# Booking more time for every transfer in a list scheduler that orders a decoder trunk's instructions

## The chip, the cores and the metric

The kernel runs on one core of a Trainium2 chip. The metric is the device time of one launch in microseconds (us). Three timed runs of the kernel before gave 1246.37, 1246.60 and 1246.83 us; the median is 1246.6 us.

## The reference

One inference step of a two-layer decoder trunk with width 1024, on a prompt of 512 tokens and on 8 sequences of 8 sample tokens, all in float32:

```python
for l in range(DEPTH):                                     # DEPTH = 2
    sh1, sc1, g1, sh2, sc2, g2 = ada_mod(c, ada_w[l], ada_b[l], 6)
    h = modulate(rms_norm(x, norm_g[l, 0]), sh1, sc1)
    if l < N_A_LAYERS:                                     # layer 0
        out, nbuf, h_last = recurrent_block(h, ...)
    else:                                                  # layer 1
        q = apply_partial_rope((h @ attn_w_q[j]).reshape(...), pos)
        out = sliding_sink_attention(q, k_all, v_all, attn_sinks[j], p0) @ attn_w_o[j]
    x = x + g1[:, None, :] * out
    h = modulate(rms_norm(x, norm_g[l, 1]), sh2, sc2)
    x = x + g2[:, None, :] * swiglu(h, ffn_w_in[l], ffn_w_out[l])
    if l == N_A_LAYERS - 1:                                # shared keys and values, once
        hk = modulate(rms_norm(x, kv_norm_g), kv_shift, kv_scale)
        kv = (hk @ w_kv).reshape(B, T, 2, N_KV_HEADS, HEAD_DIM)
        ...
y = rms_norm(x, final_g)
```

`swiglu(h, w_in, w_out)` is `(silu(gate) * up) @ w_out` with `gate, up` the halves of `h @ w_in`; its inner width is 2816. `ada_mod` turns the conditioning vectors into shifts, scales and gates. The outputs are the normalised streams, the new convolution and recurrent states and the key/value windows.

## The kernel before, in words

**Tiling.** The stream is held transposed, features on the 128 partitions. It is cut into two halves of 288 columns: 256 prompt tokens and 32 sample tokens each. A weight block of 128 x 128 stays in TensorE (PE) while 288 columns pass. Each float32 product is made of three passes: the weight is split into a rounded part (hi) and the rest (lo), the activation likewise, and PE takes hi x hi, hi x lo and lo x hi.

**The way of a weight.** SyncE (SP) issues the load of a piece into one of four buffers `raw` (NRAW = 4, L62). ScalarE (ACT) casts it into a tile `wh` (hi); VectorE (DVE) subtracts that from `raw` into `wh` (lo): `wh<-raw` is the cast and `wh<-raw,wh` the subtraction. Then PE multiplies. A `raw` buffer comes free when the last reader of it is done, and only then can the next load into that buffer be issued.

**The feed-forward part.** Most gate and up columns are computed by a scheme with seven products in place of eight (`seven`, L1435), named "11", "12", "22", "S1" to "S4"; for S1, S2 and S4 GpSimd (POOL) first adds or subtracts pieces in `raw`. Each product accumulates in a bank of PSUM (tiles `mm`, six of them). When "S2" has been accumulated DVE adds an older product to the bank and copies it to a tile `td`; when "S3" has been accumulated in the same bank DVE adds it to another `td`; only after that may PE begin "22" in that bank. The products with the second weight follow: `out`, L1494, eight pieces per group, whose loads are `raw<-in_ffn_w_out_dram`.

**What sets the order.** The kernel's functions run once without emitting anything. A recorder notes each operation with its engine, tiles and an estimated cost (`Engine.record`, L446), and `Recorder.schedule` (L240) then plays all of them through as a list scheduler: on each engine it takes, among the first waiting operations (LOOK = 24) and those within WIN = 600 places of the oldest one, the one that is ready earliest with some weight on its place in the program. The instructions are emitted in that order, once and for all; every engine executes its own list strictly in order and waits on semaphores for the others. The order of emission also decides which freed buffer a new tile gets. So the scheduler's booked times are never executed: they only decide who stands ahead of whom. For a transfer the scheduler keeps one queue, `dma_free`, which opens at OFF; a transfer holds it for its bytes and counts as landed some time after its last byte:

```python
b = max(s + op.cost + 650, dma_free[0])
dma_free[0] = b + op.lat
op.end = b + op.lat + (1700 if op.i >= self.strict else 1000)
```

(L404 to L406, in ns.) `rec.strict` is the number of operations recorded for the first loads (L2029); what is recorded behind them belongs to the later stages. While an engine of the start has nothing to do, the scheduler fills PE with transposes of the identity (`keep_busy`, L1556, tile `mm2`).

In the profile every recorded instruction has the line of the recorder's one emitting helper, L505, so that the tiles, not the lines, tell what an instruction is.

Of the kernel before, what the change touches and what calls it, by code (L numbers as in the profile page):

```python
# [12 lines left out]
F32 = mybir.dt.float32  # L13
F32R = mybir.dt.float32r
BF16 = mybir.dt.bfloat16
AF = mybir.ActivationFunctionType
# [10 lines left out]
HP = 256  # L27
# [37 lines left out]
XB = 100  # L65
NFILL = 60
AE = 100
ME = 30
YG = 6
OFF = 2300.0  # L70
AF_ = (1, 2, 4, 4)
NSL, NTA, NTB, NTD = 37, 7, 8, 4

# [70 lines left out]
class Recorder:  # L144
# [95 lines left out]
    def schedule(self):  # L240
# [64 lines left out]
        while n_left:  # L305
# [92 lines left out]
            if op.lat:  # L398

                free[e] = s + op.cost  # L400
                if e == "POOL":
                    op.end = s + op.cost + (3000 if op.i < self.strict else 5000)
                else:
                    b = max(s + op.cost + 650, dma_free[0])  # L404
                    dma_free[0] = b + op.lat
                    op.end = b + op.lat + (1700 if op.i >= self.strict else 1000)  # L406
            else:
                op.end = free[e] = s + cost
            for n in op.tiles:
# [122 lines left out]
def trunk_kernel(ctx, tc, a):  # L532
# [106 lines left out]
    def x_turn(t):  # L639
        src = xt[t].f  # L640
        if t < 4:
            for q in range(2):
                pt = aux()
                for k in range(4):
                    c = 4 * q + k
                    T.transpose(pt[:, k * P : (k + 1) * P], src[:, c * P : (c + 1) * P], ident[:])
                dst = x[t // 2][:, 4 * q : 4 * q + 4, (t % 2) * P : (t % 2) * P + P]
                (V.tensor_copy, S.copy)[q](dst, pt.rearrange("p (k n) -> p k n", k=4))
        else:
            pt = aux()  # L650
            for c in range(4):
                T.transpose(pt[:, c * P : (c + 1) * P], src[:, c * P : (c + 1) * P], ident[:])
            for h in range(2):
                V.tensor_copy(x[h][:, :, HP:HC].rearrange("p (q c) n -> p q c n", q=2), pt.rearrange("p (c q n) -> p q c n", c=4, q=2)[:, :, :, 32 * h : 32 * h + 32])
        xt[t].done()
# [199 lines left out]
    def mp(g, c):  # L855
        return mods[:, g, c, 0:1]
# [54 lines left out]
    def modulated(h, gsc, gsh, how, cs=slice(0, KC), xn=None, known=False):  # L911

        batch, se, ne, ve, le = how.split()
        pick = {"V": V, "G": G}
        for c in range(cs.start, cs.stop):
            if (c - cs.start) % int(batch) == 0:
                modulated_samples(h, gsc, gsh, pick[se], slice(c, min(c + int(batch), cs.stop)), xn, known)
            t, u = xn[c] if xn else ta(), tb()
            n, v = t.f[:, 0:HP], u.f[:, 0:HP]
            hi, lo = [h4r(h)[:, c, i, 0:HP] for i in range(2)]  # L920
            if not known:
                pick[ne[c % len(ne)]].tensor_tensor(n, x[h][:, c, 0:HP], rstd[h][:, 0:HP], ALU.mult)
            w = ve[c % len(ve)]
            if w == "S":
                S.activation(v, n, AF.Identity, bias=mp(gsh, c), scale=mp(gsc, c))
            else:
                V.tensor_scalar(v, n, mp(gsc, c), mp(gsh, c), ALU.mult, ALU.add)
            if w == "F":
                S.activation(hi, n, AF.Identity, bias=mp(gsh, c), scale=mp(gsc, c))
            else:  # L930
                S.copy(hi, v)
            pick[le[c % len(le)]].tensor_tensor(lo, v, hi.bitcast(F32), ALU.subtract)
            if not xn or known:
                t.done()
            u.done()
        if known:
            xn[KC].done()
# [85 lines left out]
    def h4r(h):  # L1023
        return H[h].r.rearrange("p (c s n) -> p c s n", c=KC, s=2)
# [962 lines left out]
    def x_half(h):  # L1987
        st = tst[h]
        for t in ((0, 1, 4), (2, 3))[h]:

            r = raws() if h else None
            w = r.f if h else x[1].rearrange("p c n -> p (c n)")[:, D * (t % 2) : D * (t % 2 + 1)]
            n, y = (512, tst[1][:, 2:3]) if t == 4 else (D, st[:, t % 2 : t % 2 + 1])
            src, dst = xt[t].f[:, 0:n], w[:, 0:n]
            if t % 2 == 0:
                S.activation(dst, src, AF.Square, accum_out=y)
            else:
                V.tensor_tensor_reduce(out=dst, in0=src, in1=src, op0=ALU.mult, op1=ALU.add, scale=1.0, scalar=0.0, accum_out=y)
            if h:
                r.done()  # L2000
            if t == 4:
                V.tensor_copy(tst[1][0:64, 5:6], y[64:128])
                V.tensor_tensor(y[0:64], y[0:64], tst[1][0:64, 5:6], ALU.add)
                V.tensor_scalar(tst[0][0:32, 2:3], y[0:32], 1.0 / D, EPS, ALU.mult, ALU.add)
                V.tensor_scalar(tst[1][32:64, 2:3], y[32:64], 1.0 / D, EPS, ALU.mult, ALU.add)
        V.tensor_scalar(st[:, 0:2], st[:, 0:2], 1.0 / D, EPS, ALU.mult, ALU.add)
        spread(h, 32 * h)
        for t in ((0, 1, 4), (2, 3))[h]:
            x_turn(t)
# [45 lines left out]

    stages.append(jobs)
    stages.append(ffn1)
    pace = [0.0]

    def do(j, h):  # L2060
        for u in j.need:
# [121 lines left out]
```

## Time and profile before

| | us |
|---|---|
| median of the timed runs | 1246.6 |
| the profiled execution's own time | 1247.9 |
| its span, first to last instruction | 1246.1 |
| PE busy | 1232.9 |
| DVE busy | 897.3 |
| ACT busy | 653.3 |
| POOL busy | 465.4 |

The mean granted TensorE clock was 0.998. All times inside the span are counted from its first instruction. A row of a timeline gives start, length, engine, operation, output<-inputs and how many instructions of that kind follow each other; in brackets stands the idle time ahead of it and what ended it. The length of a row is from the first start to the last end, and neighbouring matmuls overlap, so the distance from one start to the next is the better measure there.

### The profile page before, as it was taken

Reading aid. Unit: us, or ns where it says so; the run is one execution under the profiler, and the core shown is the slowest. Engines: PE = TensorE matmul, PEld = TensorE weight load, DVE = VectorE, ACT = ScalarE, POOL = GpSimd, SP = SyncE. Lnnn points to the kernel's source line nnn. Section 1 sums busy time; section 2 is a strip of 40 time slices with the busy share of each in tenths; the row PEclk is TensorE's granted clock in tenths of the full one; section 3 lists DMA queues with packets and bytes.
Section 4 is the critical chain, followed back from the end, with each engine's and each line's share of the span. In section 5 each row is a group of like instructions: output and inputs, shape, how many; then the busy total and the mean of one; then the engine's idle time right before and its main releaser. Section 6 shows DMA issues by size and latency. Waiting matters only on the chain.

```text
span 1246.1 us, 25373 instructions
## 1 busy us (share of the span) xinstructions
PE 1232.9 (99%) x9590; PEld 1171.4 (94%) x9590; DVE 897.3 (72%) x2137; ACT 653.3 (52%) x1461; POOL 465.4 (37%) x645
## 2 busy tenths in 40 slices
PE   8999999999999999999999999999999999999997
PEld 7888989999999999998999988999999999999997
DVE  6998875895674786477578888568767667747766
ACT  5678954852452444145367679448425435525533
POOL 3264540163441452246125445100436246335500
PEclk9999999999999999999999999999999999999999
DMA  9985554326556555445433321422332323323222
GB/s 310 300 274 173 179 167 139 124 76 212 170 189 200 170 171 165 165 142 155 118 90 69 70 61 46 122 71 100 99 103 69 112 76 102 102 85 86 85 86 76
DMA packets 221164, 165.39 MB, mean 133 GB/s; under 512 B 23817, under 2 KB 205993, under 8 KB 221010
## 3 DMA queue, kind: packets, MB, share of 16 engines
q1 hardware_dynamic: 220434, 163.39, 43.1%
q8 instruction: 75, 1.23, 0.4%
q0 software_dynamic: 608, 0.39, 0.1%
q14 instruction: 47, 0.39, 0.1%
HBM read 160.85 MB, written 4.87 MB: 133 GB/s over the span
## 4 chain that ended last, share of the span: by engine, by line
PE 92%; DVE 3%; DMA 2%; ACT 1%; POOL 1%; issue 0%; SPq 0%; DVEq 0%; ACTq 0%
PE mm L505 87%; PE ada L505 5%; DVE sl L505 1%; DVE ta L505 1%; DMA reg<-in_x_prompt_dram 1%; DMA raw<-in_rnn_w_in_dram 1%; DMA wh<-in_ada_w_dram 1%; DVE wh L505 0%; DMA raw<-in_ffn_w_out_dram 0%; POOL td L505 0%; DVE h L505 0%; DVE x L505 0%; ACT wh L505 0%; SPq L505 0%; DVE tb L505 0%
## 5 line engine op out<-in xcount | busy, mean ns | idle before, releaser
L505 PE MATMUL mm<-h,wh 128*128 128x288 f32 x4080 | 584.1, 297 | 0.3
L505 PEld LDWEIGHTS mm<-h,wh 128*128 128x128 f32 x4080 | 553.0, 188 | 12.1 <-issue 6.0
L505 PE MATMUL mm<-sl,wh 128*128 128x288 f32 x3237 | 464.2, 296 | 0.3 <-ACT sl L505 0.3
L505 PEld LDWEIGHTS mm<-sl,wh 128*128 128x128 f32 x3237 | 439.8, 188 | 6.1 <-issue 5.0
L505 ACT CAST wh<-raw 128x512 fp32r<-128x512 f32 (+3 forms) x394 | 270.5, 706 | 304.2 <-PE mm L505 188.2
L505 DVE TENSOR_TENSOR wh<-raw,wh 128x512 fp32r<-128x512 f32 (+3 forms) x396 | 362.1, 935 | 58.4 <-ACT wh L505 53.9
L505 POOL TENSOR_TENSOR raw<-raw 128x512 f32<-128x512 f32 x78 | 115.2, 1477 | 175.5 <-DVE wh L505 157.9
L505 DVE SCALAR_TENSOR_TENSOR x<-mm,mods,x 128x256 f32<-128x256 f32 x160 | 77.3, 483 | 124.6 <-PE mm L505 123.8
L505 POOL TENSOR_TENSOR x<-x,ta 128x32 f32<-128x32 f32 x120 | 41.6, 347 | 241.1 <-DVE ta L505 241.1
L505 POOL TENSOR_TENSOR raw<-raw,raw 128x512 f32<-128x512 f32 x78 | 116.1, 1488 | 4.6
L505 PE MATMUL mm<-tb,wh 128*128 128x288 f32 (+1 forms) x500 | 92.7, 299 | 1.3 <-DVE td L505 1.3
L505 POOL TENSOR_TENSOR td<-td,td 128x288 f32<-128x288 f32 x39 | 33.1, 850 | 135.8 <-ACT td L505 121.3
L505 PEld LDWEIGHTS mm<-tb,wh 128*128 128x128 f32 x500 | 74.5, 188 | 4.3 <-DVE td L505 2.9
L505 ACT ACTIVATE ta<-x 128x288 f32<-128x288 f32 (+1 forms) x56 | 24.4, 442 | 63.4 <-POOL x L505 40.4
L505 PE MATMUL mm<-ta,wh 128*128 128x288 f32 (+1 forms) x259 | 57.4, 297 | 0.0
L505 DVE TENSOR_TENSOR td<-mm,td 128x288 f32<-128x288 f32 x78 | 34.4, 452 | 21.6 <-PE mm L505 21.0
L505 DVE TENSOR_TENSOR sl<-td,sl 128x288 fp32r<-128x288 f32 x65 | 41.2, 637 | 8.9 <-ACT sl L505 8.9
L505 PE MATMUL ada<-reg,cz 128*32 128x512 f32 (+1 forms) x408 | 47.0, 547 | 0.0
L505 PEld LDWEIGHTS mm<-ta,wh 128*128 128x128 f32 x259 | 42.8, 188 | 1.0 <-ACT ta L505 1.0
L505 ACT ACTIVATE td<-td 128x288 f32<-128x288 f32 x39 | 17.3, 443 | 44.2 <-DVE td L505 44.2
L505 ACT ACTIVATE ta<-ta,stat 128x256 f32<-128x256 f32 (+2 forms) x72 | 32.5, 473 | 10.8 <-DVE stat L505 10.4
L505 ACT COPY ta<-mm 128x288 f32<-128x288 f32 (+1 forms) x51 | 19.1, 376 | 36.2 <-PE mm L505 35.1
(221 smaller groups left out, 1243.9 us busy)
## 6 DMA issues: line engine op xcount, KB each, us to landing
raw<-in_ffn_w_in_dram SPq DMA_DIRECT2D x88, 512.0 KB
reg<-in_ada_w_dram SPq DMA_DIRECT2D x72, 512.0 KB
raw<-in_ffn_w_out_dram SPq DMA_DIRECT2D x32, 384.0 KB
raw<-in_ffn_w_out_dram SPq DMA_DIRECT2D x32, 320.0 KB
reg<-in_kv_ada_w_dram SPq DMA_DIRECT2D x14, 512.0 KB
raw<-in_rnn_w_in_dram SPq DMA_DIRECT2D x13, 512.0 KB
wh<-in_ada_w_dram SPq DMA_DIRECT2D x24, 256.0 KB
raw<-in_rnn_w_out_dram SPq DMA_DIRECT2D x8, 512.0 KB
```

What stands on the lines that cost most here:

```text
L505: self.rec.add(eng, lambda: getattr(obj, name)(*map(real, args), **{k: real(v) for k, v in kw.items()}), cost, outs, ins, func, lat, port, ...
```

## The change

Two numbers of the scheduler's model of transfers change. The time booked between the last byte and the landing rises from 1000 to 2000 ns for the first loads and from 1700 to 2900 ns for all that is recorded after them, and the queue opens at 1800 instead of 2300 ns. The other edits add settings whose values leave the recorded operations as they were: `XE = "VSVS"` names the engines that the fixed pair named, `c >= FU` with FU = 8 never holds, `t > SQ` with SQ = 3 holds for t = 4 alone, which was even already, and `A0` is 0.0 as the constant was.

```diff
-OFF = 2300.0
+OFF = 1800.0
...
                     b = max(s + op.cost + 650, dma_free[0])
                     dma_free[0] = b + op.lat
-                    op.end = b + op.lat + (1700 if op.i >= self.strict else 1000)
+                    op.end = b + op.lat + (2900 if op.i >= self.strict else 2000)
...
-                dst = x[t // 2][:, 4 * q : 4 * q + 4, (t % 2) * P : (t % 2) * P + P]
-                (V.tensor_copy, S.copy)[q](dst, pt.rearrange("p (k n) -> p k n", k=4))
+                (V.tensor_copy if XE[t // 2 * 2 + q] == "V" else S.copy)(dst, pt.rearrange("p (k n) -> p k n", k=4))
...
+            if c >= FU and not xn:
+                t = ta()
...
-            if t % 2 == 0:
+            if t % 2 == 0 or t > SQ:
...
-    pace = [0.0]
+    pace = [A0]
```

The computation, its tiles and its transfers are the same; PE gets two more idle-fill transposes at the start. What changes is the order on the engines' lists: at the start on PE, then in stretches of the first layer's feed-forward part and a few single places later. In the changed kernel the recorder's helper has line 509.

At the start one PE instruction changes places with eight: the transpose of the `ada_b` vector (`mm9<-ident,sl1`), which stood behind the transposes of the first tile of the prompt (`mm4`, `mm5`), now stands ahead of them.

The first place in the feed-forward part is on DVE, where the lo parts of the pieces raw42 to raw44 are made. `wh90` to `wh95` are operands of the seven products, `wh97` is the lo part of raw44, the first piece of the second weight. Before:

```order
L505 TENSOR_TENSOR wh90_3898<-raw43_3841,wh90_3898 128x512
L505 TENSOR_TENSOR ta114_3718<-ta114_3718,mm136_3741 128x288
L505 TENSOR_TENSOR sl135_3940<-td41_3738,sl134_3919 128x288
L505 TENSOR_TENSOR td43_3827<-mm138_3845,td43_3827 128x288
L505 TENSOR_TENSOR wh91_3944<-raw43_3841,wh91_3944 128x512
L505 TENSOR_TENSOR td44_3904<-mm137_3795,td44_3904 128x288
L505 TENSOR_TENSOR sl137_3977<-ta114_3718,sl136_3933 128x288
L505 TENSOR_TENSOR ta115_3758<-ta115_3758,mm138_3845 128x288
L505 TENSOR_TENSOR wh92_3980<-raw42_3778,wh92_3980 128x512
L505 TENSOR_TENSOR wh94_3960<-raw43_3841,wh94_3960 128x512
L505 TENSOR_TENSOR wh95_4000<-raw42_3778,wh95_4000 128x512
L505 TENSOR_TENSOR wh97_4029<-raw44_3849,wh96_3911 128x640
```

And now:

```order
L509 TENSOR_TENSOR wh90_3917<-raw43_3843,wh90_3917 128x512
L509 TENSOR_TENSOR wh97_3938<-raw44_3851,wh96_3927 128x640
L509 TENSOR_TENSOR td43_3829<-mm138_3847,td43_3829 128x288
L509 TENSOR_TENSOR sl137_3963<-ta114_3720,sl136_3935 128x288
L509 TENSOR_TENSOR td44_3904<-mm137_3797,td44_3904 128x288
L509 TENSOR_TENSOR wh91_3966<-raw43_3843,wh91_3966 128x512
L509 TENSOR_TENSOR ta115_3760<-ta115_3760,mm138_3847 128x288
L509 TENSOR_TENSOR wh94_3984<-raw43_3843,wh94_3984 128x512
L509 TENSOR_TENSOR wh92_4005<-raw42_3780,wh92_4005 128x512
L509 TENSOR_TENSOR wh95_4029<-raw42_3780,wh95_4029 128x512
```

The conversion of raw44 moved from the end of this stretch to right behind that of `wh90`. By the addresses of the buffers in the built programs the load of raw46 goes into raw43's place in the kernel before and into raw44's place in the changed one (raw47 into raw42's before and raw43's now).

The second place is on ACT a little later, where raw46 and raw47 are cast (`wh100`, `wh102`). Before:

```order
L505 CAST wh92_3980<-raw42_3778 128x512
L505 CAST sl140_3992<-ta115_3758 128x288
L505 CAST wh95_4000<-raw42_3778 128x512
L505 COPY td45_4008<-mm140_3984 128x288
L505 CAST sl138_4016<-td43_3827 128x288
L505 ACTIVATE ta117_4049<-mm139_3879 128x288
L505 CAST wh100_4078<-raw46_4023 128x640
```

And now:

```order
L509 CAST sl140_3995<-ta115_3760 128x288
L509 CAST wh92_4005<-raw42_3780 128x512
L509 COPY td45_4012<-mm140_3986 128x288
L509 CAST wh100_4018<-raw46_3953 128x640
L509 CAST wh95_4029<-raw42_3780 128x512
L509 ACTIVATE ta117_4037<-mm139_3881 128x288
L509 CAST sl138_4046<-td43_3829 128x288
```

The cast of raw46 now stands ahead of the cast of `wh95`, which PE needs soon after.

The third place is on DVE again, where the banks of the seven products are emptied (`mm141`; the last of these rows to read that bank with `td45` is what "22" waits for). Before:

```order
L505 TENSOR_TENSOR mm141_4003<-mm141_4003,ta116_3938 128x288
L505 COPY td46_4062<-mm141_4003 128x288
L505 TENSOR_TENSOR td46_4062<-mm140_3984,td46_4062 128x288
L505 TENSOR_TENSOR wh101_4091<-raw46_4023,wh100_4078 128x640
L505 TENSOR_TENSOR td45_4008<-mm141_4003,td45_4008 128x288
L505 TENSOR_TENSOR wh103_4112<-raw47_4032,wh102_4095 128x640
```

And now:

```order
L509 TENSOR_TENSOR wh101_4074<-raw46_3953,wh100_4018 128x640
L509 TENSOR_TENSOR mm141_4020<-mm141_4020,ta116_3941 128x288
L509 COPY td46_4086<-mm141_4020 128x288
L509 TENSOR_TENSOR wh103_4099<-raw47_4014,wh102_4082 128x640
L509 TENSOR_TENSOR td46_4086<-mm140_3986,td46_4086 128x288
L509 TENSOR_TENSOR td45_4012<-mm141_4020,td45_4012 128x288
```

Before, the conversion of raw46 stood between the two last readers of the banks. Now it stands ahead of all of them, and the conversion of raw47 has come ahead of the two that empty `mm140` and `mm141`.

On PE, in the same stretch, products of `mm142` (raw44's) and `mm139` have come forward between those of the seven products, which puts "S3" and "22" some six matmuls later than their neighbours before.

More of the change, by code (lines that the diff above doesn't have):

```diff
@@ L67 @@
 AE = 100
+A0 = 0.0
+FU = 8
+SQ = 3
+XE = "VSVS"
 ME = 30
 YG = 6
-OFF = 2300.0
+OFF = 1800.0
 AF_ = (1, 2, 4, 4)
@@ L917, in modulated @@
                 modulated_samples(h, gsc, gsh, pick[se], slice(c, min(c + int(batch), cs.stop)), xn, known)
+            hi, lo = [h4r(h)[:, c, i, 0:HP] for i in range(2)]
+            if c >= FU and not xn:
+                t = ta()
+                n = t.f[:, 0:HP]
+                V.scalar_tensor_tensor(n, x[h][:, c, 0:HP], mp(gsc, c), rstd[h][:, 0:HP], ALU.mult, ALU.mult)
+                S.activation(hi, n, AF.Identity, bias=mp(gsh, c))
+                V.scalar_tensor_tensor(lo, n, mp(gsh, c), hi.bitcast(F32), ALU.add, ALU.subtract)
+                t.done()
+                continue
             t, u = xn[c] if xn else ta(), tb()
             n, v = t.f[:, 0:HP], u.f[:, 0:HP]
-            hi, lo = [h4r(h)[:, c, i, 0:HP] for i in range(2)]
             if not known:
```

## The prediction, blind

> **What bounds the kernel now.** I began with the span and the shares of the engines and of the chain that ended last, then went to a table by stage, then to the waits of PE, and last to the chain and the timelines around the one wait that is left. From the page:
>
> ```profile
> span 1246.1 us, 25373 instructions
> PE 1232.9 (99%) x9590; PEld 1171.4 (94%) x9590; DVE 897.3 (72%) x2137; ACT 653.3 (52%) x1461; POOL 465.4 (37%) x645
> PE 92%; DVE 3%; DMA 2%; ACT 1%; POOL 1%; issue 0%; SPq 0%; DVEq 0%; ACTq 0%
> ```
>
> PE is busy 99% of the span, so only PE's idle time, 13.2 us in all, is there to be won. The stages show where it lies (columns: stretch, its length, busy time and instructions of PE, PEld, DVE, ACT, POOL; granted clock, DMA share, GB/s; the last row is of PE alone):
>
> ```profile
> 0.00:10.00 10.00, 7.43 (x49) 6.89 (x50) 2.47 (x8) 4.77 (x9) 2.58 (x16) 1.00 0.80 221
> 30.00:40.00 10.00, 8.96 (x113) 7.88 (x112) 8.29 (x30) 6.49 (x15) 1.11 (x2) 1.00 1.10 336
> 270.00:290.00 20.00, 18.73 (x141) 18.49 (x140) 14.95 (x25) 10.15 (x20) 8.19 (x6) 1.00 0.51 158
> 830.00:1236.00 406.00, 406.00 (x3063) 404.66 (x3063) 290.05 (x598) 189.84 (x388) 146.12 (x146) 1.00 0.30 89
> 1236.00:1246.10 10.10, 3.42 (x28) 2.99 (x27) 4.42 (x16) 2.50 (x6) 0.00 (x0) 0.73 0.33 117
> 48.00:1236.00 1188.00, 1185.81 (x9072) 1.00 0.41 125
> ```
>
> The first 40 us wait for the first transfers, the last 10 for the last operations behind PE. Between 48 and 1236 us PE idles 2.19 us (1188.00 less 1185.81), 1.27 of them in the 20 us from 270 on. In the last large stage a matmul takes 406.00/3063 = 0.1326 us; that is the step to hold other stretches against.
>
> The timeline of PE there shows one wait, and the chain what led to it:
>
> ```profile
> 282.91 1.73 PE L505 MATMUL mm<-sl,wh 128*128 128x288 f32 x12
> 285.92 0.67 PE L505 MATMUL mm<-tb,wh 128*128 128x288 f32 x3 [1.27 <-DVE td L505]
> ...
> 275.98 2.31 DVE wh L505 x2
> 278.38 0.35 issue
> 278.74 5.09 DMA raw<-in_ffn_w_out_dram
> 283.91 0.74 ACT wh L505
> 284.67 0.27 DVE wh L505
> 285.41 0.46 DVE td L505
> 285.92 4.12 PE mm L505 x29
> ```
>
> Twelve matmuls from 282.91 are over at 282.91 + 12 x 0.1326 = 284.50; product "22" begins at 285.92, so 1.42 us are lost. It waits for the bank that `td45<-mm141` empties on DVE. That instruction isn't late of itself: it stands behind the conversion of raw46 (`wh101`), which waits for ACT's cast, which waits for a transfer that was issued only when DVE had converted `wh92` and `wh94` and raw43's buffer was free. So a load that PE needs much later blocks, through DVE's order, a bank that PE needs now.
>
> **The change part by part.** Nothing is computed or transferred otherwise; what counts is who stands ahead of whom.
>
> (1) *The load of raw46 leaves earlier.* The lo conversion of raw44 has moved ahead on DVE, and raw46 takes raw44's place. The rows of ACT, then of DVE:
>
> ```profile
> 269.13 0.62 ACT L505 CAST wh<-raw 128x512 fp32r<-128x512 f32 x1 [5.49 <-DMA raw<-in_ffn_w_in_dram]
> 270.21 0.73 ACT L505 CAST wh<-raw 128x640 fp32r<-128x640 f32 x1 [0.45 <-DMA raw<-in_ffn_w_out_dram]
> 270.84 0.43 ACT L505 CAST sl<-td 128x288 fp32r<-128x288 f32 x1
> 276.54 0.62 ACT L505 CAST wh<-raw 128x512 fp32r<-128x512 f32 x1
> ...
> 270.64 0.46 DVE L505 TENSOR_TENSOR ta<-ta,mm 128x288 f32<-128x288 f32 x1 [0.17 <-PE mm L505]
> 275.90 3.72 DVE L505 TENSOR_TENSOR wh<-raw,wh 128x512 fp32r<-128x512 f32 x4
> 282.06 0.46 DVE L505 TENSOR_TENSOR td<-mm,td 128x288 f32<-128x288 f32 x1
> 284.67 0.82 DVE L505 TENSOR_TENSOR wh<-raw,wh 128x640 fp32r<-128x640 f32 x1 [2.15 <-ACT wh L505]
> ```
>
> `wh90` is cast at 269.13, raw44 at 270.21. With the short cast that now stands ahead of `wh90` (0.43), ACT is through with both by about 271.4. DVE's `ta114` starts at 270.64, as PE releases it; then come `wh90` and `wh97`, each 0.7 to 0.8 us: raw44's buffer is free at about 272.4, where raw43's was free at 278.29 (275.98 + 2.31). SP has nothing else ahead of raw46's load (the loads up to raw49 stand in the same order), and needs 0.45 from the release to the start of the transfer (278.29 to 278.74): start 272.8, and with the measured 5.09, landing 277.9 in place of 283.83.
>
> (2) *What then stands where.* ACT reaches raw46's cast at about 277.5, when it is through with what now stands ahead of it (the copy `td45`, for a bank that PE finishes at about 277); it waits 0.4 us for the landing, casts until 278.6 and `wh95` until 279.3, which was done at 277.16. DVE takes `wh95`, `wh99` and two `sl` until about 281.5, then raw46's conversion until 282.3 and the addition in `mm141`. Raw47 goes into raw43's place, free at about 277.5 when `wh94` is done, lands at about 282.5 and is cast by 283.3 and converted by 284.1. Then come the two evictions, at 284.1 and, when "S3" is done, near 285.3. With six matmuls moved ahead of it, "S3" runs from about 283.5 to 285.1 and "22" is due at 285.9; its bank is free at about 285.85. So the 1.42 us go, and what takes their place is a near tie: 0 to 0.3 us. The lost time can come back up to the 1.42 if the transfer of raw47 is later than reckoned by that much, since its conversion still stands ahead of both evictions.
>
> (3) *Two smaller places.* On DVE an eviction has come ahead of a conversion at two later points. PE's rows there:
>
> ```profile
> 439.11 1.74 PE L505 MATMUL mm<-h,wh 128*128 128x288 f32 x12
> 440.89 0.66 PE L505 MATMUL mm<-tb,wh 128*128 128x288 f32 x3
> ...
> 464.65 1.74 PE L505 MATMUL mm<-h,wh 128*128 128x288 f32 x12
> 466.42 0.66 PE L505 MATMUL mm<-tb,wh 128*128 128x288 f32 x3
> ```
>
> Twelve steps are 1.59, and 1.78 and 1.77 pass: 0.19 and 0.18 lost, together 0.37, between 0 and 0.37 to be won.
>
> (4) *Conversions that come later.* Behind 290 us the price of the longer booking is that some conversions stand a place or more further back. The nearest of them to its use (that of `wh180`, one place back behind an eviction of 0.44) is done in the first row and used in the second:
>
> ```profile
> 440.76 0.67 DVE L505 TENSOR_TENSOR wh<-raw,wh 128x512 fp32r<-128x512 f32 x1
> 444.17 0.57 PE L505 MATMUL mm<-tb,wh 128*128 128x288 f32 x3
> ACT wh L505 <- PE mm L505: 188.2, 78, 6.6
> SPq L505 <- DVE wh L505: 697.2, 128, 20.9
> ```
>
> Cover: 444.17 less 441.43 is 2.74 us, against 0.44 (1.2 if one takes the added booking itself as the delay). Casts wait for PE to release their tiles (188.2 us, 78 times) and loads wait for conversions (697.2 us), so the supply runs ahead of PE and follows it: this costs 0, and what PE wins early isn't given back in waiting for weights. Without the cover each would cost its delay. The three later places where SP's loads change order are behind the same cover.
>
> (5) *The start.* The transpose of `ada_b` now stands ahead of the eight of the first tile, and waits for its vector. PE's rows, then the chain's:
>
> ```profile
> 5.45 1.04 PE L505 MATMUL mm<-ident,reg 128*128 128x128 f32 x8
> 7.17 0.23 PE L505 MATMUL mm<-ident,sl 16*128 16x16 f32 x1 [0.68 <-DMA sl<-in_ada_b_dram]
> ...
> 11.18 8.19 DMA reg<-in_x_prompt_dram
> 28.61 7.99 DMA raw<-in_rnn_w_in_dram
> ```
>
> PE stands from 5.45 to 7.17, 1.7 us, and then does the eight. Two more idle transposes add about 0.2 to 0.4. The tile's copies are 1.7 to 2 us later at 8 us, but the chain goes through transfers that end at 19.37 and 36.60, and SP's list is unchanged there; PE fills with idle transposes until then. Cost: 0, with 1.7 if the cover were gone, and as much as 0.5 to be won or lost by the shift of the later jobs in the first 48 us, which no row tells. I take 0.2 lost.
>
> *The booking itself.* The old numbers booked for such a load 460 + 650 + its bytes (936 ns) + 1700 = 3.75 us from SP's start to the landing, the new ones 4.95; measured were 0.35 + 5.09 = 5.44. So the new number is nearer to what this place took. The Trainium skill, in DMA: Bandwidth & Descriptors, under Anatomy of one DMA, fits a transfer on the GpSimd path as 2.0 us fixed plus bytes over 436 GB/s. By that an estimate for these 327,680 bytes is 2.75 us, the old booking would have been too long already and the change would go the wrong way; raw46 would land at 275.5 and raw47 at 280.7, the near tie in (2) would vanish and the sum would be 0.2 us lower. This case's row of 5.09 us, on SP's path, doesn't bear it out.
>
> **The sum.** Lost time removed: 1.42 + 0.37 = 1.79. Added: 0.1 for the near tie, 0.2 for the start. Net 1.5: span 1246.1 less 1.5 = 1244.6, and with the 1.8 us that lie around the span (1247.9 less 1246.1) a profiled execution of 1246.4. The median of the timed runs is 1.3 below the profiled execution, so 1246.6 less 1.5 = **1245.1 us**. From the bounds, 0.6 to 2.3 won (the smaller with 0.3 at the tie, 0.5 at the start and none of (3); the larger with 0.5 won at the start): 1244.3 to 1246.0.
>
> **The rivals.**
> - *The wait stays under another name.* Raw47's conversion still stands ahead of the evictions; if its transfer starts 1.4 us later than reckoned (`wh94` needs POOL's subtraction in the same buffer, and in the row of four conversions above each takes 0.93, not the 0.7 reckoned), PE waits as long as before. For it: the bank is reckoned free only 0.05 us ahead of its use. Against it: the 1.4 us. Time: 1246.6, within 0.6.
> - *Slower: raw46 blocks ACT.* Its cast now stands ahead of that of `wh95`, which PE needs at about 280.7. If raw46 lands after about 278.9, PE waits for each microsecond more; if its load were issued at 278.74 as before, it would land at 283.83, and PE would lose 4.9. Less the 1.42 and (3)'s 0.37, plus 0.2 at the start: 3.3 slower, 1249.9. For it: one transfer's time of 5.09 from which the landing is reckoned, with 1.0 to spare; transfers of the same stage could take longer. Against it: the place of raw44's conversion on DVE is fixed and 6 us earlier.
> - *The start decides.* With 1.7 us lost there, 1246.8.
> - *More than reckoned.* If also the other idle time between 48 and 1236 us (2.19 less 1.27 = 0.92) and part of the 1.04 of the slice 30 to 40 went: 1246.6 less 3.3 = 1243.3. Nothing in the order says so.
>
> **How the numbers follow.** The forecast 0.57; the wait that stays 0.22; raw46 blocking ACT 0.09; the start 0.06; more than reckoned 0.06. What a measurement here can tell from no change is 0.2%, 2.5 us. The forecast, the staying wait and the start lie within that, 0.85, less 0.02 for their edges and for the start turning out worse; faster is the last rival and an edge, 0.07; slower the blocked cast and an edge, 0.10; the same 0.83. The range reaches from 1244.0 to 1247.6: it holds the forecast, the staying wait and the start, and leaves out most of the other two, 0.15 to 0.18. The likeliest one's own range is 1244.3 to 1246.0.
>
> **What would show it.** In the profile of the changed kernel: the transfer of raw46 near 272.8 in place of 278.74; ACT's cast of it near 278 and no PE wait at `wh95` (280.7); "22" on PE without a bracket of 1.27 us near 286; starts at the two later places 1.59 after those of the twelve ahead; PE idle of some 1.7 us from 5.4 and yet the same start of the recurrent stage near 38 us; a span of 1244 to 1245. Wrong would be: a PE wait for ACT's `wh` or for `td` at 280 to 287, a first steady PE row after 38.5 us, or any PE wait over 0.5 us behind 290.

## The result and the profile after

The changed kernel takes **1243.91 us** (median of ten runs, 1243.22 to 1245.33) against 1246.65 of the kernel before (ten runs beside it, 1246.18 to 1247.19). The ratio is 0.9978, with a 95% interval of 0.9970 to 0.9986: 2.7 us faster, at the edge of what a measurement of this kernel can tell from no change (0.2%). The forecast was 1245.1 with a range from 1244.0: the direction and the main cause were right, the size was not, and the time lies 0.1 us below the range. The profiled execution took 1243.53 us.

From the page of the changed kernel, its span, the busy times and the chain that ended last:

```profile
span 1241.8 us, 25378 instructions
PE 1230.7 (99%) x9592; PEld 1170.2 (94%) x9592; DVE 894.2 (72%) x2137; ACT 654.3 (53%) x1461; POOL 469.5 (38%) x645
PE 97%; DMA 1%; DVE 1%; ACT 0%; SPq 0%; issue 0%; DVEq 0%
```

The chain now runs through PE for 97% of the span, where it was 92%: DVE's 3% are down to 1%. The stage of the one large wait, from the timelines of PE, ACT, DVE and SP of the changed kernel:

```profile
283.58 1.74 PE L509 MATMUL mm<-sl,wh 128*128 128x288 f32 x12
285.16 0.59 PE L509 MATMUL mm<-tb,wh 128*128 128x288 f32 x3
...
276.60 0.40 ACT L509 COPY td<-mm 128x288 f32<-128x288 f32 x1
276.90 1.45 ACT L509 CAST wh<-raw 128x640 fp32r<-128x640 f32 x2
...
270.23 1.42 DVE L509 TENSOR_TENSOR wh<-raw,wh 128x512 fp32r<-128x512 f32 x2
284.57 0.46 DVE L509 TENSOR_TENSOR td<-mm,td 128x288 f32<-128x288 f32 x1 [0.93 <-PE mm L509]
...
271.68 0.37 SPq L509 DMA_DIRECT2D raw<-in_ffn_w_out_dram  x1
```

Product "22" starts at 285.16, 1.58 us after the twelve matmuls ahead of it, which is twelve steps and no wait. The lo conversions of `wh90` and raw44 are done at 271.65 (270.23 + 1.42), SP takes up raw46's load then, and ACT casts raw46 at 276.90 right behind the copy `td45`, without waiting for the landing. The eviction that "22" needs now waits for PE (0.93), not PE for it.

The load went out alone, nearly 5 us ahead of the next. The share of the DMA engines in forty slices of 0.125 us, from 271.5 on, shows its bytes:

```profile
DMA  0000000000357997999522000000000000000000
```

The last of its packets ends at 274.30, 2.6 us after SP took the load up; the prediction had reckoned 5.09 for it.

The waits of PE between 48 and 1236 us, in the changed kernel and in a second profile of the kernel before (columns: us in total, times, longest):

```profile
PE mm L509 <- ACT ta L509: 0.2, 1, 0.2
```

```profile
PE mm L505 <- DVE td L505: 1.0, 1, 1.0
PE mm L505 <- ACT sl L505: 0.3, 1, 0.3
PE mm L505 <- DVE acc L505: 0.2, 1, 0.2
```

### The profile page after: what moved, and what is told of

It reads as the page before. It is cut to its first block, busy times and chain, and to the rows that moved or that the text cites. A ratio compares the mean times of both kernels' runs of the same rounds, so it can differ in the third digit from the quotient of the medians.

```text
span 1241.8 us, 25378 instructions
## 1 busy us (share of the span) xinstructions
PE 1230.7 (99%) x9592; PEld 1170.2 (94%) x9592; DVE 894.2 (72%) x2137; ACT 654.3 (53%) x1461; POOL 469.5 (38%) x645
## 4 chain that ended last, share of the span: by engine, by line
PE 97%; DMA 1%; DVE 1%; ACT 0%; SPq 0%; issue 0%; DVEq 0%
PE mm L509 91%; PE ada L509 5%; DMA reg<-in_x_prompt_dram 1%; DMA wh<-in_ada_w_dram 0%; DVE h L509 0%; SPq L509 0%; DVE sl L509 0%; DVE tb L509 0%; DVE x L509 0%; DVE wh L509 0%; ACT wh L509 0%; DVE ta L509 0%; DVE mm L509 0%; ACT h L509 0%; ACT x L509 0%
## 5 line engine op out<-in xcount | busy, mean ns | idle before, releaser
L509 POOL TENSOR_TENSOR x<-x,ta 128x32 f32<-128x32 f32 x120 | 44.1, 367 | 239.8 <-DVE ta L509 237.6
L509 ACT CAST sl<-td 128x288 fp32r<-128x288 f32 x65 | 28.0, 433 | 20.1 <-POOL td L509 12.3
```

The lines of the kernel that those rows point to most:

```text
L509: self.rec.add(eng, lambda: getattr(obj, name)(*map(real, args), **{k: real(v) for k, v in kw.items()}), cost, outs, ins, func, lat, port, ...
```

## The experiments

One table ahead, with what all runs gave. Each kernel's median and ratio are against the kernel before on the same chip (medians of 1247.09 beside the first four, 1247.22 beside the next four, 1246.65 beside the last four). The last column is PE's idle time from 264 to 291 us, the stage of the large wait, from the table by stage.

| run | median, us | ratio, 95% interval | PE idle, 264 to 291 |
|---|---|---|---|
| e1 before again | 1246.97 | 1.0000 (0.9991 to 1.0009) | 1.01 |
| e2 later loads' booking alone | 1244.40 | 0.9979 (0.9970 to 0.9987) | 0 |
| e3 opening and first loads alone | 1247.12 | 1.0000 (0.9992 to 1.0009) | 1.37 |
| e4 raw44 by hand | 1246.19 | 0.9994 (0.9985 to 1.0003) | 0.36 |
| e5 evictions first | 1246.05 | 0.9988 (0.9979 to 0.9996) | 0.55 |
| e6 raw44 back | 1245.63 | 0.9989 (0.9980 to 0.9998) | 0.86 |
| e7 raw44 by hand, in place | 1246.26 | 0.9993 (0.9984 to 1.0002) | 0.41 |
| e8 one ACT instruction more | 1246.74 | 0.9997 (0.9988 to 1.0005) | 1.29 |
| e9 five by hand | 1246.66 | 0.9998 (0.9989 to 1.0006) | 0.94 |
| e10 booking of 2300 | 1243.98 | 0.9976 (0.9966 to 0.9986) | 0 |
| e11 booking of 5000 | 1249.56 | 1.0021 (1.0012 to 1.0030) | 0 |
| e12 changed kernel again | 1243.91 | 0.9976 (0.9968 to 0.9985) | 0 |

The medians scatter too much to tell the parts of 2.7 us apart; the traces do better. The second table gives the time between the same two matmuls in each profile, less that in e1, worked out from their starts (e1's own times of the marks in the first row); e11, whose order differs from early on, is not in it. Where nothing was changed it repeats within 0.1 us, but for the start and for the stretches from 259 to 487, in which executions of one order differ by up to 0.3 (0.28 to 404, 0.26 to 454, 0.31 to 487). Of the four executions that have the order of the kernel before from 259 to 404 (the first profile, e1, e3, e8) e1 was the fastest there, by 0.23 to 0.30, so a gain in that column is larger and a loss smaller by as much against the other three. A wait also costs more than PE's idle time ahead of it, because the matmuls next to it start further apart: e6 and e9 idle less than e1 from 264 to 291 and yet take 0.50 longer to 404.

| us, less e1 | to 46.5 | to 168 | to 183 | to 259 | to 404 | to 454 | to 487 | to 645 | to 774 | to 829 | to 990 | to 1237 | all |
|---|---|---|---|---|---|---|---|---|---|---|---|---|---|
| before, first profile | 0.41 | 0.00 | -0.02 | -0.02 | 0.28 | 0.26 | -0.04 | -0.05 | 0.00 | -0.01 | 0.06 | 0.06 | 0.94 |
| e3 | 0.32 | -0.01 | -0.01 | 0.00 | 0.30 | -0.05 | -0.31 | -0.04 | 0.00 | -0.04 | 0.00 | 0.00 | 0.17 |
| e8 | 0.07 | -0.01 | -0.31 | -0.02 | 0.23 | 0.00 | -0.11 | -0.03 | 0.02 | -0.29 | -0.02 | -0.03 | -0.51 |
| e4 | -0.33 | 0.00 | -0.01 | -0.02 | -0.36 | -0.04 | -0.31 | -0.05 | 0.01 | -0.29 | -0.03 | 0.00 | -1.42 |
| e7 | -0.01 | 0.00 | -0.01 | -0.04 | -0.27 | 0.05 | -0.10 | -0.03 | -0.01 | -0.29 | -0.01 | 0.01 | -0.73 |
| e9 | -1.03 | 0.00 | -0.03 | -0.03 | 0.50 | -0.02 | 0.07 | -0.08 | 0.05 | -0.30 | 0.00 | -0.07 | -0.93 |
| e5 | 0.32 | 0.02 | -0.01 | -0.03 | -0.46 | 0.15 | -0.09 | -0.03 | 0.02 | -0.30 | 0.02 | -0.04 | -0.43 |
| e6 | -0.69 | -0.03 | -0.29 | -0.03 | 0.50 | -0.16 | -0.46 | -0.36 | 0.06 | -0.35 | 0.03 | -0.28 | -2.06 |
| e2 | 0.02 | -0.12 | -0.26 | 0.00 | -1.35 | -0.07 | -0.37 | -0.21 | 0.03 | -0.34 | 0.27 | -0.03 | -2.43 |
| e10 | -0.61 | 0.01 | -0.30 | -0.01 | -1.38 | 0.20 | -0.50 | -0.28 | 0.06 | -0.28 | 0.04 | -0.21 | -3.26 |
| changed kernel | -0.01 | -0.04 | -0.30 | -0.02 | -1.43 | -0.16 | -0.46 | -0.37 | 0.04 | -0.37 | 0.05 | -0.35 | -3.43 |
| e12 | -0.11 | -0.01 | -0.31 | -0.02 | -1.43 | -0.16 | -0.46 | -0.36 | 0.06 | -0.34 | 0.04 | -0.23 | -3.32 |

### e1, e2, e3: which part of the change

e1 is the kernel before, unchanged. e2 and e3 split the change:

```diff
 e2
-                    op.end = b + op.lat + (1700 if op.i >= self.strict else 1000)
+                    op.end = b + op.lat + (2900 if op.i >= self.strict else 1000)
 e3
-OFF = 2300.0
+OFF = 1800.0
...
+                    op.end = b + op.lat + (1700 if op.i >= self.strict else 2000)
```

> The kernel before once more, for a second profile of it. The first profiled execution (1247.9 us) lay 1.3 us above the median of the timed runs. If that was an accident of one execution, this one shows a span near 1244.9, with the 1.27 us wait near 286 and the two small losses near 440 and 466 as before, and other values for the wait of 1.04 us near 38, the 0.25 near 175 and the 0.17 near 829, which then belong to the execution and not to the order. If they are part of the order they stand again with the same size.

> Only the booking of the later loads is raised (1700 to 2900 ns); opening of the queue and the booking of the first loads as before. Theory A (all of the gain comes from the order in the feed-forward part): the whole gain, 1243.9 us, no PE wait near 286, the starts after the twelve matmuls near 440 and 466 on time. Theory B (about 1 us of the gain comes from the new order at the start): 1245.0.

> Only the opening of the queue (1800) and the booking of the first loads (2000 ns) are changed; this moves one PE instruction at the start (the transpose of ada_b, ahead of eight others) and two ACT instructions. Theory A: no change, 1246.6 us, and the wait of 1.27 us near 286 is there. Theory B: 1245.6, with PE at the same instruction some 1 us earlier at 48 us than in the second profile of the kernel before.

e2 gave 1244.40, half way between what the two theories expected; its ratio, 0.9979 against 0.9978 of the whole change, is theory A's, and e3, with a ratio of 1.0000, decides for it: the booking of the later loads carries the gain, and the start adds none that can be measured. e1 showed which of the small times belong to one execution. From its PE timeline near 440 and 465, and, last, from that of e3, whose order there is the same:

```profile
438.45 1.74 PE L505 MATMUL mm<-h,wh 128*128 128x288 f32 x12
440.03 0.59 PE L505 MATMUL mm<-tb,wh 128*128 128x288 f32 x3
...
463.72 1.76 PE L505 MATMUL mm<-h,wh 128*128 128x288 f32 x12
465.53 0.66 PE L505 MATMUL mm<-tb,wh 128*128 128x288 f32 x3
```

```profile
464.30 1.74 PE L505 MATMUL mm<-h,wh 128*128 128x288 f32 x12
465.88 0.58 PE L505 MATMUL mm<-tb,wh 128*128 128x288 f32 x3
```

In e1 the 0.19 near 440 is not there (440.03 less 438.45 is 1.58), the one near 465 is (1.81); in e3 neither is. So these two losses come and go in one and the same order: the prediction's third part counted as a property of the order what the first profile happened to show. The losses near 174 and 828, which e1's list of waits shows as 0.3 and 0.2, stood in all three profiles of that order.

The start scatters too. This row closes the start of e9, and that of the first profile of before, whose start has the same order:

```profile
36.36 0.33 PE L516 MATMUL ada<-ident,td 128*128 128x128 f32 x1
```

```profile
37.89 0.33 PE L505 MATMUL ada<-ident,td 128*128 128x128 f32 x1 [1.04 <-ACT td L505]
```

1.5 us lie between two executions of one order, as much as the forecast's whole sum.

### e4, e7, e9: raw44's conversion by itself

All three start from the order of the kernel before and move recorded operations behind others by hand (2978 is DVE's lo conversion of raw44, 2863 that of `wh90`, 2901 `sl135`; 2862, 2977 and 2900 are ACT's casts of `wh90`, raw44 and `sl134`; 2877 is POOL's subtraction in raw43):

```diff
-    order_ = rec.schedule()
+    order_ = behind(rec.schedule(), MOVES)
 e4
+MOVES = [(2978, 2863)]
 e7
+MOVES = [(2978, 2901)]
 e9
+MOVES = [(2862, 2900), (2977, 2862), (2863, 2901), (2978, 2863), (2877, 2978)]
```

> The order of the kernel before, with one instruction moved by hand: DVE's lo conversion of raw44 stands behind that of wh90, 8 places earlier. Theory A1 (that conversion frees the buffer for raw46, whose late load blocked the bank): the load of raw46 starts near 272.5 in place of 278.7, the PE wait near 286 is gone, 1.4 us gained, 1245.2 us. Rival A2 (the wait goes because the evictions themselves, or PE's products, have moved): the PE wait stays, 1246.6 us.

> The order of the kernel before, with the conversion of raw44 moved ahead by 6 places, behind ta114 and sl135 as it stands in the changed kernel, not directly behind wh90. Theory: neither the wait of 0.35 us near 273.5 that the first hand-made order brought, nor the one near 285; 1.3 us gained against the kernel before, twice what the first gained in this stretch. Rival: the eviction td43 still comes late and 0.3 to 0.6 us are lost near 273.5 to 277.5 as there.

> The order of the kernel before, with five instructions moved by hand to the places that they have in the changed kernel: on ACT the short cast sl134 ahead of those of wh90 and raw44, on DVE the conversions of wh90 and raw44 behind ta114 and sl135, on POOL the first subtraction in raw43 behind them. Theory: in the two hand-made orders before, raw44's conversion ran beside POOL's subtraction in raw43 and took 1.66 and 1.92 us instead of some 0.75, which made the eviction td43 late; with the conversion of wh90 (on which POOL waits) directly ahead of raw44's it runs alone, there is no wait near 273.5 and none near 285, and 1.2 to 1.4 us are gained against the kernel before between 258 and 335 us. If the collision isn't the reason: again 0.2 to 0.6 gained.

In all three the wait before "22" is gone. e4's PE timeline, with its DVE and POOL rows:

```profile
273.54 0.66 PE L516 MATMUL mm<-tb,wh 128*128 128x288 f32 x3 [0.35 <-DVE td L516]
283.07 1.74 PE L516 MATMUL mm<-sl,wh 128*128 128x288 f32 x12
284.65 0.58 PE L516 MATMUL mm<-tb,wh 128*128 128x288 f32 x3
...
269.99 1.66 DVE L516 TENSOR_TENSOR wh<-raw,wh 128x640 fp32r<-128x640 f32 x1 [0.41 <-ACT wh L516]
269.66 1.30 POOL L516 TENSOR_TENSOR raw<-raw 128x512 f32<-128x512 f32 x1 [0.88 <-DVE wh L516]
```

"22" starts 1.58 us after its twelve: so theory A1 holds, the early place of that one conversion removes the wait, and neither the moved evictions nor PE's new order is needed for that. But only 0.36 of 1.4 us are won in the stretch to 404 (some 0.6 against the other three executions of that order), because a new wait stands at 273.54, and a loss of 0.3 at 277.5: the conversion, 0.8 us elsewhere, took 1.66 beside POOL's subtraction, and the eviction behind it came late. e7 put it behind `sl135` and met the next subtractions:

```profile
273.88 0.67 PE L516 MATMUL mm<-tb,wh 128*128 128x288 f32 x3 [0.40 <-DVE td L516]
271.54 1.92 DVE L516 TENSOR_TENSOR wh<-raw,wh 128x640 fp32r<-128x640 f32 x1
271.38 3.21 POOL L516 TENSOR_TENSOR raw<-raw,raw 128x512 f32<-128x512 f32 x2
```

The expectation for e7 was wrong and its rival right. e9 took all five operations over, and the collision is gone, as expected, but not the loss:

```profile
269.95 1.42 DVE L516 TENSOR_TENSOR wh<-raw,wh 128x512 fp32r<-128x512 f32 x2
270.72 1.80 POOL L516 TENSOR_TENSOR raw<-raw 128x512 f32<-128x512 f32 x1 [2.65 <-DVE wh L516]
273.21 1.24 DVE L516 TENSOR_TENSOR wh<-raw,wh 128x512 fp32r<-128x512 f32 x1 [1.47 <-ACT wh L516]
277.66 0.40 PE L516 MATMUL mm<-tb,wh 128*128 128x288 f32 x1 [0.56 <-DVE wh L516]
```

```profile
271.00 1.81 POOL L509 TENSOR_TENSOR raw<-raw 128x512 f32<-128x512 f32 x1 [2.29 <-DVE wh L509]
```

Two conversions take 1.42 us, as in the changed kernel. Now POOL, which must wait for `wh90`, runs a microsecond later than in e4, DVE waits 1.47 for the operand behind it (`wh91`), and PE stands for `wh91`'s lo part and twice for `wh92`, the last time for its lo part (the PE row above); by the starts the three places cost 1.76 us against e1. In the changed kernel POOL is as late, as its row there shows, and PE doesn't wait: there the products of `mm139` and of `mm142`, raw44's own, stand between the seven products and bridge the time. The prediction had seen the products move and took them only as the cause of a near tie. No run moved these products by themselves, and they are not the only way: in e10 (below) PE's matmuls stand up to 280.8 us in the order of the kernel before, and the collision is there, yet PE doesn't wait. Its DVE row of raw44's conversion:

```profile
269.88 1.56 DVE L505 TENSOR_TENSOR wh<-raw,wh 128x640 fp32r<-128x640 f32 x1
```

There the eviction `td43` follows directly, and ACT and DVE have other instructions around it in another order too. So raw44's early conversion removes the large wait, and whether a new one takes its place hangs on the order of what stands around it, on PE or on the other engines.

### e5: the same wait, removed at its other end

```diff
+MOVES = [(3043, 3074)]
```

(DVE's conversion of raw46 behind the eviction `td45` of bank `mm141`.)

> The order of the kernel before, with one instruction moved by hand: DVE's conversion of raw46 (wh101) stands behind both evictions of the banks mm140 and mm141 instead of between them. The load of raw46 still starts near 278.3. Theory A1 (it is only DVE's order that blocks the bank): the wait of 1.0 to 1.4 us before product 22 is gone and nothing takes its place, about 1.2 us gained against the kernel before. Rival A3 (raw46 itself is too late): the wait moves to the second weight's products a few us later and nothing is gained.

PE's timeline, and from the chain of waits the transfer of raw48:

```profile
284.36 0.58 PE L516 MATMUL mm<-tb,wh 128*128 128x288 f32 x3
289.06 11.12 PE L516 MATMUL mm<-sl,wh 128*128 128x288 f32 x82 [0.55 <-ACT sl L516]
...
279.57 6.22 DMA raw<-in_ffn_w_out_dram
```

The wait before "22" is gone without any load leaving earlier: it was DVE's order that blocked the bank. Some of it comes back at 289.06, where PE waits for the split `sl`, which stands behind the casts and conversions of the late pieces (the transfer is that of the third of them, raw48): 0.46 us won in the stretch. So theory A1 and its rival A3 both have a part.

### e6: the rival that ended slower

```diff
+MOVES = [(2933, 2932), (2978, 2933), (2950, 2978)]
```

(Applied to the order of the changed kernel: raw44's conversion behind that of `wh94`; 2933 and 2950 are the loads of raw46 and raw47, moved with it so that raw46 takes the first buffer that comes free.)

> The order of the changed kernel, with one DVE instruction moved by hand: the conversion of raw44 stands behind that of wh94 again, so that raw46's load starts near 276.5, when raw43 comes free, and lands near 281.5. Everything else, ACT's cast of raw46 ahead of that of wh95 too, is as in the changed kernel. The rival of the prediction (a late raw46 blocks ACT ahead of wh95): PE waits about 3 us for wh95 near 280, about 3 us slower than the changed kernel, 1247 us. If that place on ACT does no harm: as the changed kernel, 1243.9.

From the chain, then from ACT's and PE's timelines:

```profile
275.72 3.01 DMA raw<-in_ffn_w_out_dram
...
278.81 1.25 ACT L520 CAST wh<-raw 128x640 fp32r<-128x640 f32 x2 [2.48 <-DMA raw<-in_ffn_w_out_dram]
...
278.45 0.40 PE L520 MATMUL mm<-tb,wh 128*128 128x288 f32 x1 [0.30 <-DVE wh L520]
280.84 1.60 PE L520 MATMUL mm<-h,wh 128*128 128x288 f32 x10 [0.20 <-DVE wh L520]
283.91 1.06 PE L520 MATMUL mm<-tb,wh 128*128 128x288 f32 x6 [0.28 <-DVE td L520]
```

ACT stands 2.48 us at raw46's cast with `wh95`'s behind it, and PE waits for `wh95` (280.84) and then for an eviction that DVE reaches late for the same reason (283.91). The wait at 278.45 is another one: it is for the lo part of `wh92`, ahead of which raw44's conversion now stands. So the rival's mechanism is real: with the load 4.7 us later (4.0 by the clock, in an execution that is 0.7 ahead) the stretch costs 1.93 us more than in the changed kernel (0.50 against -1.43), by the starts 0.56 of it at `wh92` and the rest at the blocked cast. By the medians, each against the kernel before beside it, it is 1.2 (1.59 won against 2.74). It was not 3 as expected, in the main since the transfer took 3.01 us and not 5.

That row corrects a reading of the prediction. The 5.09 us were not the time of one transfer: raw46, raw47 and raw48 went out within 1.5 us there, as these rows of SP in the first profile of before show, while in e6 raw46 went 1.5 us ahead of the next:

```profile
278.74 1.50 SPq L505 DMA_DIRECT2D raw<-in_ffn_w_out_dram  x3
```

```profile
275.72 0.37 SPq L520 DMA_DIRECT2D raw<-in_ffn_w_out_dram  x1
277.20 0.37 SPq L520 DMA_DIRECT2D raw<-in_ffn_w_out_dram  x1
```

The Trainium skill's fit in DMA: Bandwidth & Descriptors (Anatomy of one DMA), from which the prediction estimated 2.75 us and which it set aside, lies between the 3.01 measured for this one and the 2.6, to the last packet, of the lone load in the changed kernel. In a burst a load took 5 to 6 us here.

### e8: one instruction more on ACT

```diff
         for op in order_:
             op.emit()
+            if op.i == 0:
+                op.emit()
```

> The kernel before with ACT's first small activation issued twice, so that each later instruction of ACT stands one place further in its program; the order of the work is the same. Theory P (the losses of 0.28 us near 174 and 0.29 near 828, which were there with ACT's cast at place 317 of its program and gone with it at 318 or 319, hang on the place of the instruction in the program, not on the order of the work): both gone, 0.6 us gained, and the wait near 285 unchanged. Otherwise: no difference to the kernel before.

e8 repeats a first activation on one column. Its list of PE's waits from 48 to 1236 us has one line, and the wait before "22" is the same:

```profile
PE mm L505 <- DVE td L505: 1.3, 1, 1.3
```

The losses near 174 and 828 are gone, 0.31 and 0.29 in the second table. In the thirteen profiles of the second table the first was there when ACT's cast `sl95` stood at place 319 among ACT's instructions in the trace (counted from 0; the expectation's count, of the built program, is lower by 2) and gone at 320 and 321. The second was there when the activation `ta<-x` ahead of it stood at place 1343 and gone at 1344 and behind. ACT's row of that cast in e8, which starts 0.65 after ACT's last work, as in the changed kernel, and then in e1, where it was 0.94 (e1's row names `ta` because that update came last before the late start; the cast reads `td` in both):

```profile
173.69 0.43 ACT L505 CAST sl<-td 128x288 fp32r<-128x288 f32 x1 [0.65 <-DVE td L505]
```

```profile
173.95 0.43 ACT L505 CAST sl<-td 128x288 fp32r<-128x288 f32 x1 [0.94 <-DVE ta L505]
```

The two places lie 1024 apart, four times 256, and the traces show the period. In all fourteen profiles 1659 instructions of ACT stand directly behind a semaphore instruction after more than 0.4 us of idle time, and half of them start within 0.05 us of its end. Thirty start 0.25 to 0.45 us behind it, and 24 of these, at 0.32 to 0.34 us, stand at a place 63 above a multiple of 256, where only two more stand. So an instruction at such a place that comes after a wait starts about 0.3 us late.

So 0.6 us of the changed kernel's gain come from the place of instructions in ACT's program, which its new order shifted, and not from the order of the work. By the medians e8 gained 0.5, which its interval does not tell from nothing; the traces do. What in the chip makes the place count no run here shows.

### e10, e11, e12: how much booking

```diff
-                    op.end = b + op.lat + (1700 if op.i >= self.strict else 1000)
 e10
+                    op.end = b + op.lat + (2300 if op.i >= self.strict else 1000)
 e11
+                    op.end = b + op.lat + (5000 if op.i >= self.strict else 1000)
```

e12 is the changed kernel.

> The booking of the later loads raised by half as much (1700 to 2300 ns), the opening and the first loads as before. In the order that comes out raw44's conversion stands ahead on DVE as in the changed kernel. Theory (what counts is that place, not the size of the booking): the wait before product 22 is gone, 1244.5 us with the small losses that go with the place of ACT's instructions. Rival (half the booking, half the gain): 1245.7.

> The booking of the later loads at 5000 ns. In the order that comes out raw44's conversion stands behind those of wh91 to wh95 as in the kernel before, and raw46's conversion ahead of the eviction that product 22 waits for. Theory (the place counts): a wait of 1 to 1.4 us before product 22 is back, about 1246 us. Rival (more booking is safer): 1244 us or less.

> The changed kernel once more, for a second profile and an interval beside the same runs of the kernel before: 1243.9 us, 3 us under them, no PE wait over 0.3 us between 48 and 1236 us. If the many small differences of some nanoseconds per matmul (together 0.7 us from 530 to 645 and from 990 to 1230) belong to the kernel and not to one execution, the two profiles agree within 0.05 us in each of these stretches.

Half the booking gives the whole gain (1243.98, and -1.38 in the stretch): the size isn't what counts, but whether raw44's conversion comes forward. e11 was slower by 0.21%, but not for the reason expected. From its table by stage, then one row of its PE timeline:

```profile
48.00:264.00 216.00, 214.83 (x1605) 1.00 0.55 175
264.00:291.00 27.00, 27.00 (x207) 1.00 0.42 118
291.00:640.00 349.00, 347.93 (x2638) 1.00 0.52 165
640.00:830.00 190.00, 188.73 (x1547) 1.00 0.28 73
...
164.34 2.54 PE L505 MATMUL mm<-h,wh 128*128 128x288 f32 x17 [0.41 <-ACT td L505]
```

The wait before "22" did not come back; instead PE idles 1.2, 1.1 and 1.3 us in the three stages around, in small waits for ACT most of all. So the wait can also be avoided in an order in which raw44's conversion stays behind (there seventeen matmuls, not twelve, stand directly ahead of "22"), and too long a booking costs elsewhere.

e12 repeated the changed kernel's median, and its profile stretch by stretch within 0.12. The table by stage of PE for e1, then for e12:

```profile
48.00:1230.00 1182.00, 1180.11 (x9029) 1.00 0.41 126
830.00:1230.00 400.00, 400.00 (x3018) 1.00 0.31 90
```

```profile
48.00:1230.00 1182.00, 1181.56 (x9055) 1.00 0.42 126
830.00:1230.00 400.00, 400.00 (x3022) 1.00 0.31 90
```

In the same 1182 us the changed kernel's PE does 26 matmuls more, 3.4 us at 0.1326 each; only 1.45 of them are less idle time. The rest is what a wait costs beyond the idle time, and matmuls that follow each other a little faster. From 830 to 1230, where PE never idles in either, it does 4 more. There the distances of single matmuls differ by nanoseconds in both directions, the same way in both profiles for most; from 487 to 645 that makes 0.37 and 0.36, behind 990 0.35 and 0.23, where agreement within 0.05 was expected. The buffers of the activations and weights lie elsewhere from raw46's load on, since the order of emission decides who gets a freed one; whether that is the cause was not tried.

No kernel here beats the changed one by more than the intervals: PE idles 0.4 us between 48 and 1230.

## Why the prediction was right or wrong

- **The wait before "22"** (1.42 won): right, with its cause. The stretch gave 1.43 against e1 and 1.71 against the first profile. Raw46's load was taken up at 271.68 (reckoned 272.8), its cast ran at 276.90 (278). Two terms on the way were too long, and neither lay on PE's path: SP took the load up 0.03 us after the conversion, not 0.45, and the load took 2.6 us, not 5.09. The near tie cost nothing of its 0.1: the last eviction waited 0.93 us for PE and was done 0.13 us ahead of "22".
- **What keeps that gain**: half told. That raw44's conversion frees the buffer was right (e4). That DVE's earlier conversion collides with POOL, and that the order around it has to bridge what this makes late, was not seen. The move alone would have brought 0.3 to 0.4 against e1 (e4, e7; 0.5 to 0.7 against the other executions of that order), and the five moves of e9 a loss.
- **The two smaller places** (0.37): the size was met, 0.33 of it near 465, the cause not. e1 and e3 lack one or both with the order of the kernel before.
- **Later conversions** (0): right, no PE wait over 0.2 us from 48 us on.
- **The start** (0.2 lost): nothing that can be told from the scatter of 1.4 us there. PE waited 0.3 us for `ada_b`, not the 1.7 reckoned, and the transfers covered it.
- **The step that failed** is the sum: it held only the places where the order moves something, put the other idle time of the 1188 us (0.92) at nothing, and gave "more than reckoned" 6 in 100 because "nothing in the order says so". That rival's 1243.3 came nearest. 0.67 us came from the small losses near 174 and 828, which hang on the place of instructions in ACT's program (e8), and some 0.7 from matmuls that follow each other nanoseconds faster, whose cause stays open. Neither can be read from the order of the work. With them, 1.43 + 0.46 + 0.67 + 0.72, 3.3 of the 3.4 us between the profiles are told; the medians differ by 2.7, and with a start that scatters by more than a microsecond one pair of profiles need not show the medians' difference.
- **The profiled execution** of the kernel before lay 1.3 us above its median; the forecast subtracted a sum in one profile from the median of the runs, which was right, but e1 shows that 0.9 of that were in the start, the wait and the place near 440.
- **The rivals**: the blocked cast is real, at some 1.4 us with a load 4.7 us later (e6), and did not happen because the load left six earlier than before and took half the time reckoned. The wait that stays and the start did not happen.
- **The booking**: the prediction called 4.95 us nearer to what a transfer takes. For a load with the next 1.5 us behind it the old 3.75 was nearer (3.01 + 0.35), for a burst the new one (5.44). e10 and e11 show that nearness isn't what decided.

## What to carry to other kernels

When a kernel's bound engine idles 0.2%, a change of a list scheduler's costs is worth what it does at the one or two waits that are left; look for the instruction that stands in order ahead of what the bound engine needs, and ask what late transfer it waits for. A hand move of that one instruction removes the wait and may open another, on the operands that it makes late, unless the order around it, on the bound engine or on the others, bridges them. At this scale an order also shifts where instructions and buffers lie; here 1.4 us went that the order of the work does not explain (0.67 of them with the place of ACT's instructions), as much as with the wait itself: forecast such a change with a range that holds it, and measure from the time between the same instructions of two profiles, taken twice.

## What the runs showed of the hardware that was not expected

- Two losses of 0.3 us vanish when one small instruction is put ahead on ACT (e8): the same cast starts 0.65 in place of 0.94 us after ACT's last work. The late start comes back every 256 instructions of ACT where one stands behind a wait: 0.32 to 0.34 us in 24 of 26 cases, against 0.05 or less for half of all.
- Two profiles of the changed kernel agree within 0.12 us in every stretch of 1200 us, two of the kernel before within 0.1 in all but three (0.41, 0.28, 0.26); two orders of the same work differ by 0.3 us in stretches where PE never waits.
- A load of 320 KB took 2.6 and 2.7 us to its last packet when it went out alone (the changed kernel and e12), 3.01 to its landing with another 1.5 us behind it, and 5.09 and 6.22 in bursts in which three went out within 1.5 us.
- A subtraction on DVE that takes 0.8 us by itself took 1.56, 1.66 and 1.92 beside one on POOL (e10, e4, e7).
